# Splitting G where it is made: two fp32r parts in DRAM instead of one fp32 tile, in a Winograd feed-forward layer

## The chip, the cores and the metric

The kernel runs on one core of one Trainium2 chip. The metric is the device time of one execution in microseconds (us). Five engines work at the same time, each through its own list of instructions in order: TensorE (PE; its weight loads are shown as PEld), VectorE (DVE), ScalarE (ACT), GpSimd (POOL) and SyncE (SP), which here only starts DMA transfers. An engine waits for another only through semaphores.

## The reference

One layer of a bidirectional encoder with 1024 tokens, model width 1024 and feed-forward width 2816, all in float32:

```python
def _swiglu(x, w_in, w_out):
    g, u = jnp.split(x @ w_in, 2, axis=-1)
    return (jax.nn.silu(g) * u) @ w_out

x = x + 1/2 * post1(SwiGLU_1(pre1(x)))
u = pre_mix(x); ...            # retention and neighbourhood attention, gated and projected
x = x + post_mix(...)
x = x + 1/2 * post2(SwiGLU_2(pre2(x)))
```

pre and post are RMS norms. The change touches the two feed-forward parts (FFN 1 and FFN 2), and in them only the product of G = silu(g) * u with w_out.

## The kernel before

**Three matmuls for one.** TensorE's inputs are fp32r, a rounded float32. To keep float32 accuracy each operand X is split into a high part, ACT's cast h (L61), and a low part, VectorE's subtraction l = X - h (L62), and a product is three matmuls (`mm3`, L88 to L90): h with h, h with l, l with h. A 128x512 operand costs one ACT and one VectorE instruction to split. Weights are split by `piece` into a ring of buffers `wh`, `wl`, 8 of each.

**Seven products for eight.** Every large product is done on 2x2 blocks by Winograd's scheme: seven products of half size with sums of blocks as operands. `Winograd.NAMES` are the left operands: a11, a12, a22, s1, s2, s3, s4.

**First feed-forward product** (`ffn_in`, L405). For each of 22 feature tiles i, `Pairs.run` (L364) does seven products of 12 matmuls each, about 2.7 us a product; for the first few i two of the seven are done earlier ("leads"), so five are left: six such i in FFN 1, four in FFN 2. VectorE forms the weight sums (`t1` to `t4`, at L378, L379, L387, L396), ACT and VectorE split them into pieces, and VectorE evacuates the results and multiplies with the gate (L417) into `gt`, one tile [128, 1024] of G for a feature tile; `gt` has 3 buffers.

**Left factors** (`LeftFactors.__call__`, L430). After every second i, a pair of tiles (j of 11), POOL makes the four sums and differences of G's blocks (L440) in buffers `cmb`, 4 of them, and stores all seven left operands, 128x512 float32, 256 KB each, by DMAs from its own queue (L68) to DRAM, `gl[n][:, j * 512:(j + 1) * 512]`.

**Second feed-forward product** (`ffn_out`, L507). 7 products by 11 blocks of the feature axis are 77 steps of 12 matmuls. A step needs one block of G's left operand and one weight piece. The block comes by `Blocks`:

```python
        r = p.tile([P, 512], F32, tag="graw", name="graw", bufs=self.raws[p is not self.pools[0]])
        self.c.nc.sync.dma_start(r, src)
        a = [p.tile([P, 512], F32R, tag=g, name=g, bufs=self.pools.count(p)) for g in ("gh", "gl")]
        self.c.split(*a, r)
```

that is a load of 256 KB into one of four `graw`, and a split on ACT (`gh`) and VectorE (`gl`) into one of four pairs. The weights come as whole quadrants (`x`, 768 or 1024 KB a DMA, L521) on the same SP queue; POOL forms their differences (`sub`, L537, 55 in each FFN), and `piece` splits them. The order of the steps is written out: at step n the code asks for the operands of steps n and n + 1; how far the engines run ahead is set by the numbers of buffers. At the end of each row of blocks an epilogue (L468 to L503) normalises on ACT, VectorE and POOL beside the next steps; in FFN 1 it also transposes the result for the mixing part (tiles `pt`).

Around these the kernel has stages that the change does not touch but for the number of weight buffers: the mixing input products, attention and retention, and the output projections.

Of the kernel before, what the change touches and what calls it, by code (L numbers as in the profile page):

```python
# [10 lines left out]
F32 = mybir.dt.float32  # L11
F32R = mybir.dt.float32r
AF = mybir.ActivationFunctionType
ALU = mybir.AluOpType
# [4 lines left out]
P = 128  # L19
# [5 lines left out]
FT = DFF // P  # L25
# [13 lines left out]
class Core:  # L39
# [6 lines left out]
    def __init__(self, tc, const, wpool, psum, dram):  # L46
        self.tc, self.nc = tc, tc.nc
        self.const, self.wpool, self.psum, self.dram = const, wpool, psum, dram
        nc = self.nc
        self.ident = const.tile([P, P], F32, name="ident")  # L50
        make_identity(nc, self.ident)
        self.mhalf = const.tile([P, 8], F32, name="mhalf")
        nc.gpsimd.memset(self.mhalf, -0.5)
        self.small = None
# [19 lines left out]

    def piece(self, src, eng=None):

        h = self.wpool.tile([P, 512], F32R, tag="wh", name="wh", bufs=8)
        l = self.wpool.tile([P, 512], F32R, tag="wl", name="wl", bufs=8)
        self.split(h, l, src, eng=eng)
        return h, l  # L80

# [323 lines left out]
def ffn_in(c, pairs, pool, put):  # L405

    nc = c.nc
    for i in range(FT):
        gate = [pool.tile([P, 512], F32, tag=f"c{j}", name=f"c{j}", bufs=2) for j in range(2)]
        gt = pool.tile([P, S], F32, tag="gt", name="gt", bufs=3)  # L410
        up = gt[:, :512], gt[:, 512:]

        def done(j):
            if j < 2:
                nc.scalar.activation(gate[j], gate[j], AF.Silu)  # L415
            if j in (1, 2):
                nc.vector.tensor_tensor(up[j % 2], gate[j % 2], up[j % 2], ALU.mult)  # L417
        pairs.run(i, (*gate, *up).__getitem__, done)
        put(i, gt)


class LeftFactors:
# [1 line left out]

    order = [j + h * FT // 2 for j in range(FT // 2) for h in range(2)]

    def __init__(self, c, tmp, dst):
        self.c, self.tmp, self.dst = c, tmp, dst

    def __call__(self, i, gt):  # L430
        c, eng, j = self.c, self.c.nc.gpsimd, i // 2
        if i % 2 == 0:
            self.a11, self.a21 = gt[:, 512:], gt[:, :512]
            return
        a11, a21, a12, a22 = self.a11, self.a21, gt[:, 512:], gt[:, :512]
        s = [self.tmp.tile([P, 4, P], F32, tag="cmb", name="cmb", bufs=4).rearrange("p k t -> p (k t)")
             for _ in range(4)]
        for o, a, b, op in ((0, a21, a22, ALU.add), (2, a11, a21, ALU.subtract), (1, a22, s[2], ALU.subtract),
                            (3, a12, s[1], ALU.subtract)):
            eng.tensor_tensor(s[o], a, b, op)  # L440
        for n, a in zip(Winograd.NAMES, (a11, a12, a22, *s)):
            c.store(self.dst[n][:, j * 512:(j + 1) * 512], a)


class Blocks:


    def __init__(self, c, pools, raws):

        self.c, self.pools, self.raws, self.n = c, pools, raws, 0  # L450

    def __call__(self, src):
        p = self.pools[self.n % len(self.pools)]
        self.n += 1
        r = p.tile([P, 512], F32, tag="graw", name="graw", bufs=self.raws[p is not self.pools[0]])
        self.c.nc.sync.dma_start(r, src)
        a = [p.tile([P, 512], F32R, tag=g, name=g, bufs=self.pools.count(p)) for g in ("gh", "gl")]
        self.c.split(*a, r)
        return a


class Epilogue:
# [44 lines left out]
def ffn_out(c, tiles, q, blocks, w_out, gl, ep, side={}):  # L507
# [6 lines left out]
    later, rest, flips, xs = [], [], [], {}  # L514
# [101 lines left out]
    raws = []  # L616
# [8 lines left out]
    operands, banks, last = {}, {}, []  # L625
# [6 lines left out]
    def operand(n):  # L632
        if n < len(steps) and n not in operands:
            i, k = steps[n]
            operands[n] = blocks(gl[products[i][0]][:, k * 512:(k + 1) * 512]), c.piece(products[i][1](k))

    def one(u, k, a, b):
        c.mm3(banks[u], [p[:, u * P:(u + 1) * P] for p in a], b, k == 0, k == NK - 1)
# [1 line left out]
    for n, (i, k) in enumerate(steps):  # L640
# [11 lines left out]
        if later and i > 3:  # L652
            f = later.pop(0)
# [372 lines left out]
def trunk_layer(ctx: ExitStack, tc, x, g1a, w1i, w1o, g1b, gma, wmt, wnv, wrv, logits, dtab, rope, bias,  # L1026
# [11 lines left out]
    def dt(name, shape):  # L1038
        return dram.tile(shape, F32, name=name)

    gl = [{n: dt(f"g{i}{n}", [P, FT // 2 * 512]) for n in Winograd.NAMES} for i in range(2)]
    x1, x2 = dt("x1", [S, D]), dt("x2", [S, D])
    d = {
        "a21": dt("a21", [P, 4, 512]),
# [28 lines left out]
        fin.lead(lambda: early.tile([P, 512], F32, tag="lead", name="lead", bufs=6), on_pool=(3, 4, 5, 0))  # L1073
    g0 = pool(left, "gl10")
    with tc.tile_pool(name="fin1", bufs=1) as fp:
        ffn_in(c, fin, fp, LeftFactors(c, early, gl[0]))
    right.close()

    spool = pool(left, "s1")
# [9 lines left out]
    q = [p.tile([P, 4, 512], F32, tag="x", name="q", bufs=n) for p, n in ((ep, 2), (ep, 2), (spool, 8), (spool, 8))]  # L1089
    ahead = {}  # L1090
    fo = Epilogue(c, ep, g1b, gma, rows(x), rows(x1), wx.put)
    rest = ffn_out(c, [[b11, b12], [b21, b22]], q, Blocks(c, (g0, g1, g1, g1), (1, 3)), w1o, gl[0], fo,
                   {n: (lambda j=j: ahead.update({j: c.load_w(wnv[j])})) for j, n in enumerate((65, 66))})
    g_stack.close()
    wx.tmp = pool(g_stack, "cmb1")
# [53 lines left out]
    for f, k in zip(rest, FLIP_FILL):  # L1149
        fill(k)  # L1150
        f = f()
# [167 lines left out]


    with tc.tile_pool(name="fin2", bufs=1) as fp:
        ffn_in(c, fin, fp, LeftFactors(c, cmb, gl[1]))
    left.close()
    a_stack.close()
    g_stack.close()
# [2 lines left out]
             for _ in range(2)]  # L1328
    with tc.tile_pool(name="out2", bufs=1) as op:
        q = [op.tile([P, 4, 512], F32, tag="q", name="q", bufs=4) for _ in range(4)]  # L1330
        ffn_out(c, tiles, q, Blocks(c, (g0, g1, g0, g1), (2, 2)), w2o, gl[1],
                Epilogue(c, op, g2b, None, rows(x2), rows(out), None))
    right.close()

# [77 lines left out]
```

## Time and profile before

| what | value |
|---|---|
| median of 3 runs | 2324.83 us (2323.96 to 2324.98) |
| profiled execution | 2322.93 us, its span 2321.1 us |
| mean granted TensorE clock | 0.990 |
| TensorE busy | 2227.8 us, 96% of the span |
| VectorE / ACT / POOL busy | 1742.1 / 1003.5 / 746.3 us |
| moved by DMA | 361.25 MB, 156 GB/s on average |

Stages, in us from the start of the span: norm and leads to 69; first product of FFN 1 to 456; its second product to 690; mixing, attention, retention and output projections to 1687; first product of FFN 2 to 2087; its second product to 2313; end at 2321.

How to read the profile: a group's row gives line, engine, operation, the tiles (out<-in), shapes, count, then busy time, mean ns of one, and after the second bar the time that the engine was idle just before them with what ended it. A wait row says which engine and line waited for which, in us in total, how often, and the longest. A timeline row is start, length, engine, line, operation, tiles. A matmul of 512 columns starts about 0.23 us after the one before it.

### The profile page before, as it was taken

Reading aid. Unit: us, or ns where it says so; the run is one execution under the profiler, and the core shown is the slowest. Engines: PE = TensorE matmul, PEld = TensorE weight load, DVE = VectorE, ACT = ScalarE, POOL = GpSimd, SP = SyncE. Lnnn points to the kernel's source line nnn. Section 1 sums busy time; section 2 is a strip of 40 time slices with the busy share of each in tenths; the row PEclk is TensorE's granted clock in tenths of the full one; section 3 lists DMA queues with packets and bytes.
Section 4 is the critical chain, followed back from the end, with each engine's and each line's share of the span. In section 5 each row is a group of like instructions: output and inputs, shape, how many; then the busy total and the mean of one; then the engine's idle time right before and its main releaser. Section 6 shows DMA issues by size and latency. Waiting matters only on the chain.

```text
span 2321.1 us, 29919 instructions
## 1 busy us (share of the span) xinstructions
PE 2227.8 (96%) x10288; PEld 1837.5 (79%) x10288; DVE 1742.1 (75%) x2833; ACT 1003.5 (43%) x2102; POOL 746.3 (32%) x735
## 2 busy tenths in 40 slices
PE   6999999999998999999999999999799999999998
PEld 5788888787786887778888888887578888887776
DVE  7886666689778768869875678547887666668976
ACT  6332222353454323248885675226533233324443
POOL 5232222278424134411101222101523131316942
PEclk9999999999998999999999999999899999999999
DMA  4332323374335542257745567766433232328443
GB/s 145 116 137 101 119 94 115 131 282 152 107 114 172 175 161 100 103 177 247 221 159 176 164 217 237 283 217 213 146 114 118 96 114 95 114 88 326 120 138 122
DMA packets 135896, 361.25 MB, mean 156 GB/s; under 512 B 16000, under 2 KB 43776, under 8 KB 133632
## 3 DMA queue, kind: packets, MB, share of 16 engines
q1 hardware_dynamic: 109344, 271.76, 36.4%
q0 software_dynamic: 26400, 87.58, 10.0%
q8 instruction: 81, 1.33, 0.2%
q14 instruction: 71, 0.58, 0.1%
HBM read 263.33 MB, written 100.14 MB: 157 GB/s over the span
## 4 chain that ended last, share of the span: by engine, by line
PE 72%; DVE 13%; issue 6%; POOL 4%; DMA 3%; ACT 2%; POOLq 0%; DVEq 0%; SPq 0%; ACTq 0%
PE ps L90 22%; PE ps L88 22%; PE ps L89 22%; DVE wl L62 3%; DVE gl L62 2%; PE pt L88 1%; PE pt L89 1%; DMA wraw<-in_dram 1%; PE pt L90 1%; DVE tmp L118 1%; POOL rstd L98 1%; POOL cmb L288 1%; PE ps L741 1%; PE pt L760 1%; POOL q L482 1%
## 5 line engine op out<-in xcount | busy, mean ns | idle before, releaser
L62 DVE TENSOR_TENSOR wl<-wraw,wh 128x512 fp32r<-128x512 f32 x516 | 381.3, 762 | 79.0 <-ACT wh L61 78.1
L61 ACT CAST wh<-wraw 128x512 fp32r<-128x512 f32 x524 | 300.7, 618 | 202.9 <-DVE wraw L396 65.6
L90 PE MATMUL ps<-wh,gl 128*128 128x512 f32 x612 | 241.7, 399 | 17.0 <-DVE gl L62 16.6
L88 PE MATMUL ps<-wh,gh 128*128 128x512 f32 x612 | 240.9, 395 | 7.0 <-ACT gh L61 5.8
L89 PE MATMUL ps<-wl,gh 128*128 128x512 f32 x612 | 240.3, 394 | 2.0 <-DVE wl L62 2.0
L62 DVE TENSOR_TENSOR gl<-graw,gh 128x512 fp32r<-128x512 f32 (+2 forms) x178 | 182.7, 1030 | 74.8 <-ACT gh L61 74.7
L61 ACT CAST gh<-graw 128x512 fp32r<-128x512 f32 (+2 forms) x178 | 106.6, 601 | 210.7 <-PE ps L89 57.5
L537 POOL TENSOR_TENSOR x<-x 128x512 f32<-128x512 f32 x110 | 182.7, 1688 | 37.5 <-DMA x<-in_dram 26.7
L415 ACT ACTIVATE c<-c 128x512 f32<-128x512 f32 x88 | 55.7, 633 | 294.6 <-DVE c L385 195.2
L62 DVE TENSOR_TENSOR wl<-x,wh 128x512 fp32r<-128x512 f32 x146 | 169.2, 1169 | 7.0 <-ACT wh L61 6.9
L90 PEld LDWEIGHTS ps<-wh,gl 128*128 128x128 f32 x612 | 115.9, 190 | 52.0 <-DVE gl L62 28.5
L88 PEld LDWEIGHTS ps<-wh,gh 128*128 128x128 f32 x612 | 115.7, 189 | 34.2 <-ACT gh L61 9.3
L89 PEld LDWEIGHTS ps<-wl,gh 128*128 128x128 f32 x612 | 116.1, 190 | 26.2 <-DVE wl L62 2.7
L61 ACT CAST wh<-t 128x512 fp32r<-128x512 f32 x58 | 36.1, 622 | 200.3 <-DVE t L379 200.3
L90 PE MATMUL ps<-a12h,wl 128*128 128x512 f32 x280 | 109.9, 393 | 3.7 <-DVE wl L62 3.7
L88 PE MATMUL ps<-a11h,wh 128*128 128x512 f32 x280 | 111.8, 399 | 1.4 <-ACT wh L61 0.7
L90 PE MATMUL ps<-a11h,wl 128*128 128x512 f32 x280 | 110.6, 395 | 0.7 <-DVE wl L62 0.7
L89 PE MATMUL ps<-a11l,wh 128*128 128x512 f32 x280 | 110.6, 395 | 0.0
L88 PE MATMUL ps<-a12h,wh 128*128 128x512 f32 x280 | 110.3, 394 | 0.0
L68 POOL DMA_DIRECT2D g1a<-gt x33 | 18.1, 548 | 286.5 <-DVE gt L417 286.5
L88 PE MATMUL ps<-a22h,wh 128*128 128x512 f32 x280 | 109.7, 392 | 0.0
L89 PE MATMUL ps<-a12l,wh 128*128 128x512 f32 x280 | 109.2, 390 | 0.0
(359 smaller groups left out, 6196.6 us busy)
## 6 DMA issues: line engine op xcount, KB each, us to landing
wraw<-in_dram SPq DMA_DIRECT2D x221, 512.0 KB, 4.4
x<-in_dram SPq DMA_DIRECT2D x16, 1024.0 KB, 7.0
g0s<-cmb POOLq DMA_DIRECT2D x44, 256.0 KB, 2.7
graw<-g0s SPq DMA_DIRECT2D x44, 256.0 KB, 2.8
g1s<-cmb POOLq DMA_DIRECT2D x44, 256.0 KB, 2.7
graw<-g1s SPq DMA_DIRECT2D x44, 256.0 KB, 2.8
bt<-in_dram SPq DMA_DIRECT2D x24, 384.0 KB, 4.1
g0a<-gt POOLq DMA_DIRECT2D x33, 256.0 KB, 2.4
```

Of the source, the lines that this page charges most:

```text
L61: nc.scalar.copy(h, src)
L62: (eng or nc.vector).tensor_tensor(l, src, hf, ALU.subtract)
L88: mm(ps, a[0], b[0], start=start, stop=False)
L89: mm(ps, a[0], b[1], start=False, stop=False)
L90: mm(ps, a[1], b[0], start=False, stop=stop)
L98: self.nc.gpsimd.tensor_tensor(r[:, :n], ms, self.mhalf[:, :n], ALU.pow)
L118: nc.vector.scalar_tensor_tensor(xn[:, bs], x[:, bs], r[:, 0:1], gain[:, bs], op0=ALU.mult, op1=ALU.mult)
L288: nc.gpsimd.tensor_tensor(s3, h2, s3, ALU.subtract)
L415: nc.scalar.activation(gate[j], gate[j], AF.Silu)
L482: (eng or c.nc.gpsimd).tensor_tensor(h if out is None else out, h, self.post[:, b * 512:(b + 1) * 512], ALU.mult)
L537: e = nc.gpsimd.tensor_tensor(out, a, b, ALU.subtract).ins
L741: nc.tensor.matmul(bv, q[:, rg * P:(rg + 1) * P], k, start=n == 0, stop=n == 1)
```

## The change

`LeftFactors` splits each of the seven left operands itself: ACT copies it, rounded, into a new ring `gth` of four buffers, VectorE subtracts in place, and POOL's queue stores both parts, 14 stores a pair instead of 7, in the order a11, s1, s3, a22, s2, a12, s4. In DRAM a block of a left operand is now [128, 1024], high part and low part side by side. `Blocks` loads both parts with one DMA of 512 KB into one of seven buffers and splits nothing. The weight rings `wh` and `wl` have 7 buffers instead of 8, everywhere in the kernel.

```diff
@@ -74,8 +74,8 @@
 
     def piece(self, src, eng=None):
 
-        h = self.wpool.tile([P, 512], F32R, tag="wh", name="wh", bufs=8)
-        l = self.wpool.tile([P, 512], F32R, tag="wl", name="wl", bufs=8)
+        h = self.wpool.tile([P, 512], F32R, tag="wh", name="wh", bufs=7)
+        l = self.wpool.tile([P, 512], F32R, tag="wl", name="wl", bufs=7)
         self.split(h, l, src, eng=eng)
         return h, l
 
@@ -424,8 +424,9 @@
 
     order = [j + h * FT // 2 for j in range(FT // 2) for h in range(2)]
 
-    def __init__(self, c, tmp, dst):
-        self.c, self.tmp, self.dst = c, tmp, dst
+    def __init__(self, c, tmp, parts, dst):
+
+        self.c, self.tmp, self.parts, self.dst = c, tmp, parts, dst
 
     def __call__(self, i, gt):
         c, eng, j = self.c, self.c.nc.gpsimd, i // 2
@@ -438,25 +439,30 @@
         for o, a, b, op in ((0, a21, a22, ALU.add), (2, a11, a21, ALU.subtract), (1, a22, s[2], ALU.subtract),
                             (3, a12, s[1], ALU.subtract)):
             eng.tensor_tensor(s[o], a, b, op)
-        for n, a in zip(Winograd.NAMES, (a11, a12, a22, *s)):
-            c.store(self.dst[n][:, j * 512:(j + 1) * 512], a)
+
+        a = dict(zip(Winograd.NAMES, (a11, a12, a22, *s)))
+        for n in ("a11", "s1", "s3", "a22", "s2", "a12", "s4"):
+            h = self.parts.tile([P, 512], F32R, tag="gth", name="gth", bufs=4)
+            l = a[n].bitcast(F32R)
+            c.nc.scalar.copy(h, a[n])
+            c.nc.vector.tensor_tensor(l, a[n], h.bitcast(F32), ALU.subtract)
+            for q, p in enumerate((h, l)):
+                c.store(self.dst[n][j][:, q * 512:(q + 1) * 512], p.bitcast(F32))
 
 
 class Blocks:
 
 
-    def __init__(self, c, pools, raws):
-
-        self.c, self.pools, self.raws, self.n = c, pools, raws, 0
+    def __init__(self, c, pools):
+
+        self.c, self.pools, self.n = c, pools, 0
 
     def __call__(self, src):
         p = self.pools[self.n % len(self.pools)]
         self.n += 1
-        r = p.tile([P, 512], F32, tag="graw", name="graw", bufs=self.raws[p is not self.pools[0]])
-        self.c.nc.sync.dma_start(r, src)
-        a = [p.tile([P, 512], F32R, tag=g, name=g, bufs=self.pools.count(p)) for g in ("gh", "gl")]
-        self.c.split(*a, r)
-        return a
+        a = p.tile([P, 2, 512], F32, tag="g", name="g", bufs=self.pools.count(p))
+        self.c.nc.sync.dma_start(a.rearrange("p q t -> p (q t)"), src)
+        return [a[:, q].bitcast(F32R) for q in range(2)]
 
 
 class Epilogue:
@@ -632,7 +638,7 @@
     def operand(n):
         if n < len(steps) and n not in operands:
             i, k = steps[n]
-            operands[n] = blocks(gl[products[i][0]][:, k * 512:(k + 1) * 512]), c.piece(products[i][1](k))
+            operands[n] = blocks(gl[products[i][0]][k]), c.piece(products[i][1](k))
 
     def one(u, k, a, b):
         c.mm3(banks[u], [p[:, u * P:(u + 1) * P] for p in a], b, k == 0, k == NK - 1)
@@ -1038,7 +1044,7 @@
     def dt(name, shape):
         return dram.tile(shape, F32, name=name)
 
-    gl = [{n: dt(f"g{i}{n}", [P, FT // 2 * 512]) for n in Winograd.NAMES} for i in range(2)]
+    gl = [{n: dram.tile([FT // 2, P, 1024], F32, name=f"g{i}{n}") for n in Winograd.NAMES} for i in range(2)]
     x1, x2 = dt("x1", [S, D]), dt("x2", [S, D])
     d = {
         "a21": dt("a21", [P, 4, 512]),
@@ -1073,7 +1079,7 @@
         fin.lead(lambda: early.tile([P, 512], F32, tag="lead", name="lead", bufs=6), on_pool=(3, 4, 5, 0))
     g0 = pool(left, "gl10")
     with tc.tile_pool(name="fin1", bufs=1) as fp:
-        ffn_in(c, fin, fp, LeftFactors(c, early, gl[0]))
+        ffn_in(c, fin, fp, LeftFactors(c, early, fp, gl[0]))
     right.close()
 
     spool = pool(left, "s1")
@@ -1089,7 +1095,7 @@
     q = [p.tile([P, 4, 512], F32, tag="x", name="q", bufs=n) for p, n in ((ep, 2), (ep, 2), (spool, 8), (spool, 8))]
     ahead = {}
     fo = Epilogue(c, ep, g1b, gma, rows(x), rows(x1), wx.put)
-    rest = ffn_out(c, [[b11, b12], [b21, b22]], q, Blocks(c, (g0, g1, g1, g1), (1, 3)), w1o, gl[0], fo,
+    rest = ffn_out(c, [[b11, b12], [b21, b22]], q, Blocks(c, (g0, *[g1] * 6)), w1o, gl[0], fo,
                    {n: (lambda j=j: ahead.update({j: c.load_w(wnv[j])})) for j, n in enumerate((65, 66))})
     g_stack.close()
     wx.tmp = pool(g_stack, "cmb1")
@@ -1319,7 +1325,7 @@
 
 
     with tc.tile_pool(name="fin2", bufs=1) as fp:
-        ffn_in(c, fin, fp, LeftFactors(c, cmb, gl[1]))
+        ffn_in(c, fin, fp, LeftFactors(c, cmb, fp, gl[1]))
     left.close()
     a_stack.close()
     g_stack.close()
@@ -1328,7 +1334,7 @@
              for _ in range(2)]
     with tc.tile_pool(name="out2", bufs=1) as op:
         q = [op.tile([P, 4, 512], F32, tag="q", name="q", bufs=4) for _ in range(4)]
-        ffn_out(c, tiles, q, Blocks(c, (g0, g1, g0, g1), (2, 2)), w2o, gl[1],
+        ffn_out(c, tiles, q, Blocks(c, (g0, g1, g0, g1, g0, g1, g1)), w2o, gl[1],
                 Epilogue(c, op, g2b, None, rows(x2), rows(out), None))
     right.close()
```

## The prediction

> **What bounds the kernel now.** I read the page first, for the engine that is full and for the price of one operation; then TensorE's waits, cut at the stages that the change touches; then the windows, to see which engine stands behind each wait; then the timelines around the places where work arrives.
>
> ```profile
> span 2321.1 us, 29919 instructions
> ...
> PE 2227.8 (96%) x10288; PEld 1837.5 (79%) x10288; DVE 1742.1 (75%) x2833; ACT 1003.5 (43%) x2102; POOL 746.3 (32%) x735
> ...
> L62 DVE TENSOR_TENSOR gl<-graw,gh 128x512 fp32r<-128x512 f32 (+2 forms) x178 | 182.7, 1030 | 74.8 <-ACT gh L61 74.7
> L61 ACT CAST gh<-graw 128x512 fp32r<-128x512 f32 (+2 forms) x178 | 106.6, 601 | 210.7 <-PE ps L89 57.5
> ...
> g0s<-cmb POOLq DMA_DIRECT2D x44, 256.0 KB, 2.7
> ```
>
> TensorE is the bound, 96% busy, so the change can only win what TensorE waits for the split of G, and lose what it makes TensorE wait for elsewhere. The profiled execution took 2322.93 us, 1.8 more than its span; the median of the runs is 2324.83, 1.9 above it. I add my sum to both alike. A measurement of this kernel can tell about 0.2%, 4.65 us, from no change.
>
> TensorE's waits in the middle of the two second products (470 to 625 us, 2100 to 2250), then at their first steps (455 to 470, 2086 to 2100); columns are total, times, longest:
>
> ```profile
> PE ps L90 <- DVE gl L62: 5.6, 8, 2.1
> PE ps L88 <- ACT gh L61: 1.5, 1, 1.5
> ...
> PE ps L90 <- DVE gl L62: 7.5, 9, 2.1
> PE ps L88 <- ACT gh L61: 1.5, 1, 1.5
> ...
> PE ps L90 <- DVE gl L62: 1.3, 1, 1.3
> PE ps L88 <- ACT gh L61: 1.2, 1, 1.2
> ...
> PE ps L90 <- DVE gl L62: 1.4, 1, 1.4
> PE ps L88 <- ACT gh L61: 1.2, 1, 1.2
> ```
>
> So nothing but G's split stalls TensorE there. Windows (length; busy us of PE, PEld, DVE, ACT, POOL; granted clock, DMA share, GB/s):
>
> ```profile
> 72.00:455.00 383.00, 382.63 (x1688) 316.51 (x1687) 275.44 (x421) 118.14 (x206) 96.09 (x111) 1.00 0.33 114
> 464.00:472.00 8.00, 8.00 (x33) 6.49 (x32) 6.16 (x10) 3.83 (x7) 1.58 (x4) 0.88 1.01 396
> 480.00:560.00 80.00, 78.17 (x339) 62.77 (x339) 79.69 (x56) 37.45 (x68) 73.02 (x44) 1.00 0.59 202
> 470.00:625.00 155.00, 147.81 (x633) 118.48 (x632) 133.02 (x117) 68.68 (x129) 111.99 (x69) 0.99 0.53 176
> 2100.00:2250.00 150.00, 140.85 (x606) 112.54 (x605) 128.39 (x110) 64.42 (x118) 107.89 (x67) 1.00 0.56 188
> ```
>
> From 480 to 560 VectorE is the full engine (79.69 of 80). The first product of the FFN (72 to 455), which gets the work, leaves TensorE 0.4 us idle in 383 and VectorE 107. On averages the move is free there; the start of that stage decides.
>
> **Part 1, the split leaves the second product.** 77 casts and 77 subtractions per FFN go. What TensorE gets back is its idle time of the two middle windows: 155.00 - 147.81 = 7.2 and 150.00 - 140.85 = 9.2. Each of the 19 waits also hides 0.16, since a matmul shows 0.39 us but starts 0.23 after the last (rows at 249.49 and 249.94 below: two starts, 0.45): 3.0. And one stretch of halved clock follows a wait (chain of waits):
>
> ```profile
> 568.62 0.43 PE ps L88
> ...
> 571.18 0.43 PE pt L88
> ...
> 572.65 0.23 PE ps L90
> ```
>
> Seven matmuls from the first row to the second take 0.43 instead of 0.23: 1.4, call it 1.5. Sum 20.9. With 28 of its 56 operations gone from the 480 to 560 window, VectorE cannot fill it. What is late next is ACT, held by the epilogue's normalisation around 600 and 2230; the weight pieces, now 7 deep, cover 6 steps of 2.73 us (12 matmuls by 0.2275), 16 us. I leave 2 there: **gain 19** (bounds 10 and 21).
>
> The Trainium skill, page "TensorE: Matmul & The Clock Gate", section "Why this matters for your kernels", asks only for no idle gap over about 3 us. The longest wait ahead of the rows above is 2.1, and the clock halved all the same, so the trace decides. By the page the 1.5 would not be gained and the sum would be that much higher.
>
> **Part 2, the split arrives in the first product.** Per pair of feature tiles ACT gets 7 copies (0.60), VectorE 7 subtractions, POOL's queue 14 stores in place of 7. On average 4.2 us per 38 us on VectorE: free. But the copies go through a ring of 4 (`gth`): the sixth (a12) waits until the store of s1's high part has landed, the seventh (s4) until that of s3's has. In the order of the changed program the first pairs have these copies on ACT, and their subtractions on VectorE, ahead of the weight work that TensorE needs next. The first pair, POOL, VectorE, TensorE:
>
> ```profile
> 100.91 2.94 POOL L440 TENSOR_TENSOR cmb<-gt 128x512 f32<-128x512 f32 x2 [1.03 <-DVE gt L417]
> 103.78 0.56 POOL L68 DMA_DIRECT2D g0a<-gt  x1
> 104.36 1.30 POOL L440 TENSOR_TENSOR cmb<-gt,cmb 128x512 f32<-128x512 f32 x1
> 110.36 0.68 DVE L62 TENSOR_TENSOR wl<-t,wh 128x512 fp32r<-128x512 f32 x1
> 110.11 0.39 PE L88 MATMUL ps<-s2h,wh 128*128 128x512 f32 x1
> 111.09 0.50 PE L90 MATMUL ps<-s2h,wl 128*128 128x512 f32 x1 [0.37 <-DVE wl L62]
> ```
>
> There is no slack even now: the last row waits 0.37. After: s1 and s3 end at 103.8, s2 at 105.1; store of s1's high part, s4's subtraction, two stores (0.56 + 1.3 + 2 x 0.56) bring the store of s3's high part to 108.1; it lands 2.7 later, 110.8; copy 111.4; VectorE's subtraction 112.1; t2 112.7; its cast 113.3. TensorE wanted it at 110.11: **3.2 late**. The second pair:
>
> ```profile
> 127.25 3.00 POOL L440 TENSOR_TENSOR cmb<-gt 128x512 f32<-128x512 f32 x2 [1.18 <-DVE gt L417]
> 132.98 0.39 PE L90 MATMUL ps<-a22h,wl 128*128 128x512 f32 x1
> 138.42 0.39 PE L90 MATMUL ps<-s2h,wl 128*128 128x512 f32 x1
> ```
>
> It starts 3.2 later, 130.45. s1's store is issued 4.2 after that and lands at 137.35; copy, subtraction, one evacuation and the a22 weight's split (0.6 each) end at 139.8; wanted at 132.98 + 3.2 = 136.2: **3.6**. s3's store lands at 140.35; copy, subtraction and eight VectorE operations lead to t2's low part at about 147.0, wanted at 138.42 + 6.8 = 145.2: **1.8**. Together 8.6, and two stretches of halved clock, since waits of this size brought one above: 3. In the second FFN one early pair (subtractions from 1718.8, wanted at 1730) is late by 1 to 3: 2. **Cost 14** (bounds 6 and 18).
>
> In the steady part a pair has room:
>
> ```profile
> 229.91 3.37 POOL L440 TENSOR_TENSOR cmb<-gt 128x512 f32<-128x512 f32 x2 [1.05 <-DVE gt L417]
> 249.49 0.39 PE L88 MATMUL ps<-s2h,wh 128*128 128x512 f32 x1
> 249.94 0.39 PE L90 MATMUL ps<-s2h,wl 128*128 128x512 f32 x1
> ```
>
> By the same steps (subtractions to 235.8, three stores to 237.5, landing 240.2, copy, subtraction, three VectorE operations, cast) the cast ends at 243.9, 5.6 ahead of 249.49: no cost.
>
> **Part 3, twice the bytes, at the worst moment.** G is written and read as 512 KB a block: in the 480 to 560 window one block a step adds 0.262 MB per 2.73 us, 96 GB/s to 202; no bound. At the start of the second product the queues are full already (396 GB/s above). Issues there, 450 to 520 us, with KB and median landing; then the chain's row of the first wait:
>
> ```profile
> x<-in_dram SPq DMA_DIRECT2D x6, 1024.0 KB, 6.1
> graw<-g0a SPq DMA_DIRECT2D x9, 256.0 KB, 5.7
> g0s<-cmb POOLq DMA_DIRECT2D x4, 256.0 KB, 7.1
> ...
> 458.90 0.63 ACT gh L61
> ```
>
> The present waits of the first steps stay: block 1 lands about 1.5 later (0.262 MB more, and more behind it) and saves its split (0.60 + 0.68). New is the queue behind. Step 6 would start at 458.9 + 5 x 2.73 + 3 of waits = 475.5; its data must have left by 473.4 (2.1 of a landing is not transfer: 2.7 less 0.262 MB at 400 GB/s). By then SP must have brought blocks 1 to 6 (3.15 MB) and three weight tiles issued before (2.89): 6.03 MB. From 456.4 the queues carry 6.8, so loads alone fit. But the last pair's 13 remaining stores, 3.41 MB, come in from 461. If they take half while queued, loads carry 4.6 x 0.4 + 12.4 x 0.2 = 4.3 MB, 1.7 short: 4.6 us more at half rate, then 2 at full, 6.6 late. If loads went first: 0. Four stores landed in 7.1, that is 1.05 MB in 5 us of transfer, half of 0.4; so I stand near the upper end: 5 in each FFN. **Cost 10** (bounds 0 and 16).
>
> The Trainium skill, page "DMA: Bandwidth & Descriptors", section "Specifications", gives a core about 358 GB/s of HBM. The 396 measured is above it, so I use 400; by the page step 6 would be some 2 us later still in each FFN, and the sum 4 higher.
>
> Weight pieces 7 deep instead of 8 elsewhere: I take 0 (bounds -1 and +3), as none of the waits above names wh or wl.
>
> **Sum:** -19 + 14 + 10 = +5: profiled 2328, median **2330**.
>
> **The rivals.**
> *Loads win at the start.* Stores yield and part 3 costs nothing: -19 + 14 = -5, 2320. For it: blocks are asked for 7 ahead. Against: the 7.1 us landings.
> *The ring is free sooner.* If a store frees its buffer 1.0 us after its issue, when it has been read, and not 2.7, then each of the four delays above shrinks by up to 1.7 and part 2 costs 6: -3, 2322. For it: the copy needs the buffer, not the arrival. Against: the wait in the program is for the whole store.
> *Stores are quick*, the other side of the sign: both of these together, by one mechanism, stores that neither hold the ring nor take their half of the queue: -19 + 6 = -13, **2312**. It decides from two points: s4's copy done by 109.7 instead of 111.4, and the 13 stores behind the loads of step 6.
> *The ring stalls every pair.* If landing grows from 2.7 beyond 8.3 (2.7 + 5.6), each us past that counts once for some 18 steady pairs: one us gives +5 + 18, 2348. For it: 7.1 in the crowded stretch. Against: DMA share 0.33 from 72 to 455.
> *The middle stays bound.* G's low part is only the last of a queue behind VectorE and POOL (73 of 80 busy); then wl is late next and half the gain is lost: +14, 2339. Against: 53 subtractions leave that window.
>
> **How the numbers follow.** Forecast 0.50, loads win 0.18, ring free sooner 0.08, stores quick 0.06, every pair 0.09, middle bound 0.09. My forecast's own range is 2322 to 2338; of its 0.50 I count 0.27 slower by over 0.2%, 0.20 within, 0.03 faster. Of loads win and ring free sooner (0.26) 0.12 faster, 0.11 within, 0.03 slower; stores quick faster; the last two slower. Faster 0.21, same 0.31, slower 0.48. Range 2312 to 2346: it leaves out the far ends of "stores quick" and of "every pair".
>
> **What would show it.** Right: no TensorE wait on G's parts from 480 to 625, VectorE near 50 of 80 from 480 to 560; waits on wh or wl of 3 us near 110 and 136; waits on a G block or its weight near 470 to 480 with landings of G and its stores over 7 us. Wrong: no wait over 1 us from 100 to 150 (part 2), first steps as now (part 3), waits on wl from 540 to 570 (part 1), or waits repeating every 38 us.

## The result, and the profile after

| | median | runs | ratio to before, 95% interval |
|---|---|---|---|
| before | 2323.96 us | 9 (2320.84 to 2326.18) | |
| changed | 2333.73 us | 9 (2328.31 to 2340.19) | 1.0042 (1.003 to 1.0055) |

The changed kernel is slower by 0.42%, 9.8 us. Its profiled execution took 2335.32 us, 1.6 above its median; the span is 12.1 us longer than before's. First the page, the lines that answer to those of before:

```profile
span 2333.2 us, 30479 instructions
...
PE 2230.0 (96%) x10288; PEld 1839.0 (79%) x10288; DVE 1677.9 (72%) x2833; ACT 1010.2 (43%) x2102; POOL 806.1 (35%) x889
...
DMA packets 148220, 442.03 MB, mean 189 GB/s; under 512 B 18465, under 2 KB 46241, under 8 KB 145953
...
x<-in_dram SPq DMA_DIRECT2D x16, 1024.0 KB, 12.2
g0s<-gth POOLq DMA_DIRECT2D x44, 256.0 KB, 4.1
```

VectorE does the same 2833 instructions in 64 us less, POOL 60 us more, the DMA 81 MB more; TensorE's share is what it was. Sums of the page do not say where 12 us went. Both programs issue 10288 matmuls, in an order that differs only locally, so the k-th matmul of one can be set against the k-th of the other. The table gives, for every kernel run, how much longer than before's profile each stretch took, in us, between matmuls 200, 1900, 2200, 2700, 3100, 7700, 9300, 9600 and 10200 (first product of FFN 1; start and middle of its second product; its end; everything between the FFNs; the same of FFN 2) and from there to the end of the span.

| kernel | first 1 | start 1 | middle 1 | end 1 | between | first 2 | start 2 | middle 2 | last |
|---|---|---|---|---|---|---|---|---|---|
| changed | +11.9 | +7.5 | -14.0 | +1.4 | +7.6 | +3.1 | +1.3 | -10.1 | +3.4 |
| e1 ring free | +14.9 | +6.4 | -14.0 | +2.3 | +8.1 | +5.1 | +2.0 | -10.1 | +3.4 |
| e2 split on POOL | +15.5 | +7.3 | -14.0 | +2.5 | +3.2 | +8.6 | +0.3 | -10.1 | +3.4 |
| e3 last low parts early | +13.2 | +1.7 | -14.0 | +3.1 | +2.3 | +4.5 | +0.6 | -10.1 | +3.4 |
| e4 before, 7 buffers | -0.5 | +0.6 | -2.9 | +0.5 | +3.3 | 0.0 | -1.1 | -0.4 | 0.0 |
| e5 before, no low part | -0.7 | -2.2 | -14.2 | 0.0 | -0.6 | 0.0 | -4.5 | -9.3 | +0.1 |
| e6 no early subtraction | -0.6 | +6.4 | -14.0 | +1.3 | +7.8 | 0.0 | +1.8 | -10.1 | +3.4 |
| e7 raw pairs | -0.6 | +7.0 | -14.0 | +2.7 | +2.7 | 0.0 | +1.8 | -10.1 | +0.1 |
| e8 raw pairs and a11 | -0.6 | +4.5 | -14.0 | -0.3 | +3.9 | 0.0 | -0.4 | -10.1 | +0.1 |
| e9 the same, 8 buffers | -0.5 | +5.4 | -14.0 | -0.4 | -2.9 | +1.4 | +1.4 | -10.1 | +0.1 |
| e10 four split pairs | -0.5 | +4.7 | -13.7 | +7.6 | +3.8 | 0.0 | -0.1 | -10.1 | +4.1 |
| e11 the same, 8 buffers | 0.0 | +4.7 | -13.9 | +0.9 | -4.7 | 0.0 | +2.7 | -1.4 | +4.1 |
| e12 before again | -0.6 | +2.2 | -0.7 | -0.3 | -1.2 | 0.0 | +0.4 | 0.0 | 0.0 |

The last row is the scale: two profiles of before differ by up to 2.2 in a stretch, and by 0.1 in all. Each row is one execution, and not always a middling one: those of e1 and e6 took 7.1 and 3.8 us more than the medians of their kernels, that of e9 3.6 less. In the changed kernel the middles give back 24.1, and seven other stretches take 36.2. TensorE's waits in the changed kernel, middle of FFN 1's second product with its start (470 to 640 us):

```profile
PE ps L88 <- DMA g<-g0a: 6.4, 3, 2.6
PE ps L127 <- issue: 1.5, 1, 1.5
PE ps L88 <- ACT gth L447: 0.8, 1, 0.8
PE ps L88 <- ACT wh L61: 0.6, 1, 0.6
```

No wait on the split of a loaded block of G is left (the row with gth is the copy of the last pair); loads of G have taken its place. The window that answers to 480 to 560 of before (there VectorE was busy 79.69 of 80 with 56 operations, the queues at 202 GB/s):

```profile
490.00:570.00 80.00, 76.78 (x324) 62.98 (x325) 32.90 (x29) 21.46 (x36) 62.28 (x44) 0.96 0.90 347
```

VectorE fell to 33 of 80, with half the operations (the prediction said near 50; a weight split also got shorter, 1169 ns on average against 1334 from 470 to 625 before), and the queues went from 0.59 to 0.90 of their time. TensorE was busy 1.4 us less than before in this window, which begins inside the start with its waits on loads. In the first product of FFN 1, VectorE and then TensorE (timelines):

```profile
101.12 0.69 DVE L448 TENSOR_TENSOR gt<-gt,gth 128x512 fp32r<-128x512 f32 x1 [1.06 <-POOL cmb L441]
101.73 3.62 DVE L448 TENSOR_TENSOR cmb<-cmb,gth 128x512 fp32r<-128x512 f32 x2
105.28 0.68 DVE L448 TENSOR_TENSOR gt<-gt,gth 128x512 fp32r<-128x512 f32 x1
105.88 0.68 DVE L448 TENSOR_TENSOR cmb<-cmb,gth 128x512 fp32r<-128x512 f32 x1
106.48 0.68 DVE L385 TENSOR_TENSOR c<-ps,c 128x512 f32<-128x512 f32 x1
107.08 0.68 DVE L448 TENSOR_TENSOR gt<-gt,gth 128x512 fp32r<-128x512 f32 x1
107.68 0.68 DVE L390 TENSOR_TENSOR c<-ps,gt 128x512 f32<-128x512 f32 x1
...
110.08 0.67 DVE L448 TENSOR_TENSOR cmb<-cmb,gth 128x512 fp32r<-128x512 f32 x1
110.68 0.68 DVE L379 TENSOR_TENSOR t<-wraw 128x512 f32<-128x512 f32 x1
...
112.12 0.50 PE L88 MATMUL ps<-s2h,wh 128*128 128x512 f32 x1 [1.90 <-ACT wh L61]
...
139.70 0.79 PE L90 MATMUL ps<-a22h,wl 128*128 128x512 f32 x1 [3.57 <-DVE wl L62]
```

TensorE waits where the prediction had it wait (112 and 136 to 140). But from 105.28 on VectorE starts an operation every 0.60 us, without idle time (no brackets behind these rows): the last subtraction (110.08) and the t2 behind it (110.68) came when their turn came, not when a store had landed.

### The profile page after: what moved, and what is told of

It is laid out like the page before. It is cut to its first block, busy times and chain, and to the rows that moved or that the text cites. A ratio compares the mean times of both kernels' runs of the same rounds, so it can differ in the third digit from the quotient of the medians.

```text
span 2333.2 us, 30479 instructions
## 1 busy us (share of the span) xinstructions
PE 2230.0 (96%) x10288; PEld 1839.0 (79%) x10288; DVE 1677.9 (72%) x2833; ACT 1010.2 (43%) x2102; POOL 806.1 (35%) x889
## 3 DMA queue, kind: packets, MB, share of 16 engines
q0 software_dynamic: 38720, 127.96, 14.7%
## 4 chain that ended last, share of the span: by engine, by line
PE 59%; issue 13%; DVE 12%; POOL 6%; DMA 6%; ACT 3%; POOLq 0%; SPq 0%; DVEq 0%; ACTq 0%
PE ps L90 18%; PE ps L88 18%; PE ps L89 18%; DVE wl L62 3%; POOL cmb L441 2%; DMA g1s<-gth 1%; DMA g<-g0a 1%; PE pt L89 1%; PE pt L90 1%; PE pt L88 1%; DMA wraw<-in_dram 1%; ACT wh L61 1%; POOL rstd L98 1%; DVE tmp L118 1%; DVE t L379 1%
## 5 line engine op out<-in xcount | busy, mean ns | idle before, releaser
L62 DVE TENSOR_TENSOR wl<-x,wh 128x512 fp32r<-128x512 f32 x146 | 137.8, 956 | 192.1 <-ACT wh L61 191.0
L88 PE MATMUL ps<-wh,g 128*128 128x512 f32 x484 | 191.5, 397 | 11.3 <-DMA g<-g0a 6.4
L89 PE MATMUL ps<-wl,g 128*128 128x512 f32 x484 | 191.1, 395 | 0.0
L90 PE MATMUL ps<-wh,g 128*128 128x512 f32 x484 | 190.4, 393 | 0.0
L61 ACT CAST wh<-x 128x512 fp32r<-128x512 f32 x146 | 88.6, 620 | 216.4 <-PE pt L90 93.0
L441 POOL TENSOR_TENSOR cmb<-gt 128x512 f32<-128x512 f32 x44 | 63.7, 1464 | 320.6 <-DVE gt L417 320.6
L543 POOL TENSOR_TENSOR x<-x 128x512 f32<-128x512 f32 x110 | 158.8, 1469 | 34.2 <-DMA x<-in_dram 24.2
L88 PEld LDWEIGHTS ps<-wh,g 128*128 128x128 f32 x484 | 92.2, 191 | 33.4 <-ACT wh L61 7.4
L90 PE MATMUL ps<-a22h,wl 128*128 128x512 f32 x280 | 110.3, 394 | 3.6 <-DVE wl L62 3.6
L89 PE MATMUL ps<-a22l,wh 128*128 128x512 f32 x280 | 109.8, 392 | 0.0
L89 PEld LDWEIGHTS ps<-wl,g 128*128 128x128 f32 x484 | 92.3, 191 | 20.1 <-DVE wl L62 1.2
```

The lines of the kernel that those rows point to most:

```text
L61: nc.scalar.copy(h, src)
L62: (eng or nc.vector).tensor_tensor(l, src, hf, ALU.subtract)
L88: mm(ps, a[0], b[0], start=start, stop=False)
L89: mm(ps, a[0], b[1], start=False, stop=False)
L90: mm(ps, a[1], b[0], start=False, stop=stop)
L543: e = nc.gpsimd.tensor_tensor(out, a, b, ALU.subtract).ins
```

## The experiments

**Is it the ring?** e1 takes the ring's waits out of the early pairs, e2 takes two of the splits off ACT and VectorE.

```diff
# e1: in three early pairs the store reads the low part, not the ring's buffer
-            for q, p in enumerate((h, l)):
+            for q, p in enumerate((l if j < 3 and n in ("a11", "s1", "s3") else h, l)):
```

> The changed kernel, but in the first three pairs of each FFN the DMAs that stored the high parts of a11, s1 and s3 store the low part in their place: same bytes, same queue, but no store holds a buffer of the ring of four any more, so the copies of a12 and s4 wait for no landing (the stored values of these blocks are thereby not the high parts). Theory (the ring): the time that the first product of FFN 1 lost against before (+11.9 us by TensorE's matching instructions) falls to 0 to 4, that of FFN 2 (+3.1) to 0 to 1, the rest stays: some 10 us faster than the changed kernel. Rival (the seven added subtractions on VectorE, 4.2 us a pair, are in front of the weights): +11.9 stays at 8 or more. Second rival (twice the DMA issues on POOL's queue): stays as well.

```diff
# e2
+            if n in ("a12", "s4"):
+                eng.tensor_copy(h, a[n])                       # eng: POOL
+                eng.tensor_tensor(l, a[n], h.bitcast(F32), ALU.subtract)
+            else: ...                                          # as changed
```

> The changed kernel, with the copy and the subtraction of a12 and s4 moved from ACT and VectorE to POOL, so that only POOL's own list waits for the ring. Theory (the ring holds up ACT and VectorE in front of the weights): first product of FFN 1 from +11.9 to +1 to +4, of FFN 2 from +3.1 to 0 to +1, about 10 us faster than the changed kernel, 2321 to 2326. Rival (VectorE's five remaining subtractions do it): +8 or more stays. Price to watch: POOL's added 2 copies and 2 subtractions, about 5 us a pair of 38.

Measured: e1 2333.73 us (ratio to before 1.0047, 1.003 to 1.0064), e2 2338.68 (1.0061, 1.0045 to 1.0076). The loss in the first product of FFN 1 did not fall in either: +14.9 and +15.5. (e1's median is the changed kernel's; its profiled execution was its slowest, so that it lost more than the changed kernel is not shown.) TensorE's waits from 95 to 160 us, e1 and then e2, and a VectorE row of e2:

```profile
PE ps L88 <- ACT wh L61: 7.1, 4, 2.5
PE ps L90 <- DVE wl L62: 2.1, 2, 1.7
...
PE ps L90 <- DVE wl L62: 7.1, 2, 4.4
PE ps L88 <- ACT wh L61: 3.3, 2, 2.6
...
110.25 2.34 DVE L387 TENSOR_TENSOR wraw<-wraw 128x512 f32<-128x512 f32 x1
```

The waits are still for the weights behind VectorE. In e2 an operation of 0.68 us took 2.34 beside POOL's new subtraction: two splits fewer on VectorE cost it more than they saved. The Trainium skill, page "SBUF — State Buffer", section "SBUF: two separate sides", says that VectorE and GpSimd share a pair of ports which one operation holds to its end, when VectorE has two inputs in SBUF and GpSimd reads SBUF; this row and the 3.62 for two operations at 101.73, beside POOL's first subtractions, agree. So the ring fell as the cause in the first product.

**Is it VectorE's added work?**

e6 leaves out the seven subtractions of each of the first three pairs; what is stored as low part is the block as it is.

```diff
# e6
-            c.nc.vector.tensor_tensor(l, a[n], h.bitcast(F32), ALU.subtract)
+            if j >= 3:
+                c.nc.vector.tensor_tensor(l, a[n], h.bitcast(F32), ALU.subtract)
```

> The changed kernel, without the 7 VectorE subtractions in each of the first three pairs of each FFN (the block as it is is stored as the low part, so these blocks count double); ring, copies, stores, queue and bytes unchanged. The first two runs took the ring away and moved two splits to POOL, and the loss in the first product of FFN 1 rose from +11.9 to +14.8 and +15.6: the ring is not it. New theory (VectorE is full while five products a tile leave it 13.6 us a tile, 21 subtractions of 0.6 are 12.6 us and pass through to TensorE): loss falls to 0 to +3, in FFN 2 from +3.1 to 0 to +1. Rival (ACT's copies or POOL's 14 issues in front of the weights): +8 or more stays.

Measured: 2315.19 us (0.9963, 0.9951 to 0.9975). First product of FFN 1 -0.6, as in the second profile of before; of FFN 2 0.0 instead of +3.1. Windows from 100 to 150 us, before, changed, e6 (length; busy PE, PEld, DVE, ACT, POOL; clock, DMA share, GB/s):

```profile
100.00:150.00 50.00, 49.63 (x220) 40.76 (x219) 47.76 (x70) 17.32 (x30) 17.86 (x21) 1.00 0.45 158
...
100.00:150.00 50.00, 42.12 (x168) 32.52 (x166) 42.24 (x63) 20.01 (x35) 24.98 (x35) 0.93 0.56 202
...
100.00:150.00 50.00, 50.00 (x223) 41.40 (x222) 45.29 (x68) 24.76 (x44) 23.32 (x35) 1.00 0.61 214
```

e6 keeps the ring, the copies and all 14 stores of a pair, and loses nothing. This settles part 2: the subtractions, in a stretch in which VectorE had 2.2 of 50 us left. The expectation's 12.6 us, for 21 subtractions, is near the 11.9 by chance. In the changed kernel's timeline only 14 of them, 8.4 us at 0.60, fall in this stretch (101 to 110 and 132 to 141); those of the third pair, from 169.7 on, come after TensorE's lag has reached its 11.9. VectorE, which works in order, also stands idle ahead of each of the two groups until POOL has made its operand (1.06 us in the row at 101.12, 1.69 at 131.81). That makes 9.0 us more than it had free, an estimate from these rows. The five gaps between TensorE's matmuls that grew most grew by 8.6 in all; the other 3.3 are mostly matmuls at a lower granted clock (0.93 in the window).

**Is it the bytes at the start of the second product?** e3 moves the stores of the last pair's low parts five pairs earlier, with that pair's values.

> The changed kernel, with the low parts of the last pair not stored at the end of the first product (1.8 MB less there; the bytes are written five pairs earlier, with that pair's values, so the last block's low parts are not the right ones). Theory (stores and loads share a full queue at the start of the second product): the loss there, +7.5 us in FFN 1 against before, falls to +2 to +5; waits on loads of G near 487 and 497 shrink. Rival (the loads alone, 512 instead of 256 KB, are too many): stays at +6 or more. Second rival (the last pair's copies on ACT hold up the weights): the ring turns faster with fewer stores and some of it goes too, but the waits would name the weights' casts, not G's loads.

Measured: 2328.84 us (1.0025, 1.0016 to 1.0034); start +1.7 instead of +7.5, in FFN 2 +0.6 instead of +1.3. Landings of the changed kernel from 455 to 520, a step of its chain of waits, then TensorE's waits from 456 to 505, changed and e3:

```profile
g<-g0a SPq DMA_DIRECT2D x10, 512.0 KB, 15.8
g0s<-gth POOLq DMA_DIRECT2D x4, 256.0 KB, 10.0
...
477.13 23.11 DMA g<-g0a
...
PE ps L88 <- DMA g<-g0a: 6.4, 3, 2.6
PE ps L88 <- ACT gth L447: 0.8, 1, 0.8
...
PE ps L88 <- DMA g<-g0a: 4.1, 4, 1.4
PE ps L88 <- ACT gth L447: 0.8, 1, 0.8
```

A block of G that takes 23 us from issue to landing outruns seven blocks of prefetch (19 us). With 1.8 MB less in the queue the same block takes 18.8, the longest wait falls from 2.6 to 1.4 us, and the granted clock from 480 to 520 is 1.00 instead of 0.91. So stores do hold loads up. But with no more bytes of stores than before, G's blocks still take up to 18.8 us, against 9.2 before, and the median of g0a hardly moves (15.8 to 14.7): the larger part of the long landings goes with the doubled loads.

In FFN 2 the longest wait at the start, 2.8 us, is another one. ACT, TensorE and the ring of four at the last pair there:

```profile
2117.79 0.62 ACT L447 CAST gth<-gt 128x512 fp32r<-128x512 f32 x1 [6.88 <-DMA g1s<-gth]
2118.31 2.17 ACT L61 CAST wh<-x 128x512 fp32r<-128x512 f32 x4
...
2118.98 0.80 PE L88 MATMUL ps<-wh,g 128*128 128x512 f32 x1 [2.79 <-ACT wh L61]
```

ACT stood idle for 6.9 us until a store of a copy had landed, and the weight's cast behind it came late. This is the step that the prediction saw in the first product; it happened here, where stores are slow. No run took the ring away at the last pair alone; e1 frees it in the first three.

**What is the middle worth?** e5, on before, leaves out the subtraction that makes G's low part; the high part stands in for it.

```diff
# e5
-        a = [p.tile([P, 512], F32R, ...) for g in ("gh", "gl")]
-        self.c.split(*a, r)
-        return a
+        a = [p.tile([P, 512], F32R, ...) for g in ("gh",)]
+        self.c.nc.scalar.copy(a[0], r)
+        return a * 2
```

> The kernel before, without the subtraction that makes G's low part (the high part is used in its place, so the products are not the right ones); load, copy, eight weight buffers and all stores as before. Theory (VectorE's subtraction of G is what the middle of the second products waited for): against before -13 to -15 in the middle of FFN 1's second product and -9 to -11 in FFN 2's, as the changed kernel has (-14.0 and -10.1), and nothing lost in the first products: 2296 to 2302. Rival (the shorter chain of loads and copies did it too): less than -10 and -7. Between the FFNs it tells how far two profiles with eight weight buffers differ: if within 2 us, the 5 to 8 us that the changed kernels lose there belong to seven buffers; if 3 or more, they are scatter. The last drain of POOL stays at 4.1 us.

Measured: 2291.38 us (0.9857, 0.9842 to 0.9872). Middles -14.2 and -9.3, against -14.0 and -10.1 of the changed kernel; ACT's copy and the load are still there. So it was VectorE's subtraction alone that TensorE waited for. It is also faster at the start in FFN 2 (-4.5; the -2.2 in FFN 1 is within the scatter), which put it below the expected range.

**Do seven weight buffers cost anything?**

```diff
# e4, on before
-        h = self.wpool.tile([P, 512], F32R, tag="wh", name="wh", bufs=8)     # and wl
+        h = self.wpool.tile([P, 512], F32R, tag="wh", name="wh", bufs=7)
```

> The kernel before with 7 instead of 8 buffers in the weight rings, nothing else. The prediction took 0 (-1 to +3) for this. If it is the cause of the 7 to 8 us that the changed kernel's profile lost between the two FFNs (about +0.3 near 1000 to 1100 us, +6 between 1390 and 1500), the same loss shows in these places and the time is 5 to 10 us above before. If those were the disturbance of one run, the time is within 3 us of before and the loss is elsewhere or gone.

> The kernel before, unchanged, profiled a second time: how far two profiles of one kernel differ stage by stage. If the stretch between the FFNs differs by less than 2 us, the 3 to 8 us of the kernels with seven weight buffers are no scatter; the first products and the middles of the second products should agree within 0.5 us.

Measured: e4 2324.41 us (1.0007, 0.9998 to 1.0016): within the scatter as a whole. e12, one execution, 2322.82. But in the column "between", all nine kernels with seven buffers lose 2.3 to 8.1 us, and the five with eight stand at 0 (before), -0.6, -1.2, -2.9 and -4.7. TensorE's waits from 1000 to 1500 us, changed, then e4, then before again:

```profile
PE ps L747 <- ACT qh L64: 4.2, 1, 4.2
PE pt L766 <- DVE s L756: 3.9, 3, 2.0
PE ps L88 <- DVE sb L928: 1.8, 1, 1.8
PE pt L968 <- ACT yn L959: 1.6, 1, 1.6
...
PE pt L760 <- DVE s L750: 4.0, 3, 2.1
PE ps L741 <- ACT qh L64: 1.4, 1, 1.4
PE pt L962 <- ACT yn L953: 1.2, 1, 1.2
...
PE ps L741 <- ACT qh L64: 3.2, 1, 3.2
PE pt L760 <- DVE ptl L62: 1.6, 2, 0.8
PE pt L760 <- DVE s L750: 1.2, 2, 0.8
```

e4 differs from before by the buffers alone, and it has the changed kernel's longer waits for `s` and its wait for `yn`; so have all nine, and none of the five. None of these waits names wh or wl: why a smaller ring of weights makes `s` and `yn` late in attention and retention was not followed up. The place repeats: between matmuls 6400 and 7000 (1410 to 1532 us) all nine lose 2.6 to 6.8 us and the other four 0 to 0.3. So the buffers cost something there, 2.9 us in e4 and 6.8 in the changed kernel; the rest of the column is within what kernels with equal buffers differ by. By time alone e4 cannot tell its part from no change.

**Can it be had without the costs?** e7 stores the pairs that cost (0, 1, 2 and 10) unsplit and splits their blocks in the second product; e8 does so with a11 too; e9 is e8 with eight weight buffers.

```diff
# e7; e8 adds: or n == "a11"
+def unsplit(n, j):
+    return j in (0, 1, 2, 10)
# LeftFactors
+            if unsplit(n, j):
+                c.store(self.dst[n][j][:, :512], a[n])
+                continue
# Blocks
+        if raw:
+            self.c.nc.sync.dma_start(a[:, 1], src[:, :512])
+            self.c.split(*hl, a[:, 1])
# e9: e8 with wh, wl bufs=8, gth bufs=2, Blocks of six buffers
```

> The changed kernel, but pairs 0, 1, 2 and 10 of each FFN are stored unsplit, 7 stores, and their four blocks of each product are loaded as 256 KB and split in the second product, as before; the other seven pairs as changed. The results are the right ones. Theory (VectorE is full early, the queues are full at the last pair, VectorE has room in the middle now): first product of FFN 1 0 to +2, start of its second product 0 to +3, middle -11 to -14, in FFN 2 0, 0 to +2, -8 to -10; 5 +- 3 between the FFNs, and at the end POOL's last drain, which went from 4.14 to 7.98 us with 154 more DMAs on its queue, at 6.6 with 98 more: in all -8 to -14 against before, 2310 to 2316, faster than both. Rival (splits in the middle bring back the waits on G's low part): middle -7 and -5, 2320 or more.

> As the kernel with raw pairs, and also a11 is stored unsplit in all pairs, so that the first product of the second matmul loads 256 KB a block and splits it there, where VectorE has room and the queues have none. Theory (bytes at the start): a start another 0 to 2 us shorter than with raw pairs alone, POOL's last drain 6.2 us, 1 to 3 us faster in all. Rival (the start is at before's level already with raw pairs, and the added splits put VectorE behind): same or slower by up to 2.

> The kernel with raw pairs 0, 1, 2, 10 and a11 raw, with the weight rings back at eight buffers; the room comes from the ring of the copies, two instead of four, and from G's blocks, six deep instead of seven. Right results. Theory (seven weight buffers cost 3 to 8 us between the FFNs): that stretch from +4.0 to 0 to +2, 2 to 4 us faster than with seven; the ring of two costs nothing, as the ring of four did not. Rival (the 4.0 are scatter): the same time within 1.5. Second rival (the ring of two now holds up ACT in front of the weights): a wait in every pair from 190 us on, slower by 5 or more.

Measured: e7 2312.53 us (0.9949, 0.9936 to 0.9961), e8 2308.13 (0.9928, 0.9915 to 0.994), e9 2306.5 (0.9924, 0.991 to 0.9937). All three beat both kernels, e9 by 0.76% against before. The first products lose nothing, the middles keep all of -14.0 and -10.1 although 4 of 11 blocks are split there again. The start was expected at 0 to +3 in e7 and is +7.0. TensorE's waits from 455 to 525, e7 and then e8; then e9's window:

```profile
PE ps L90 <- DVE g L62: 4.3, 3, 2.7
PE ps L88 <- ACT g L61: 3.2, 2, 2.1
PE ps L88 <- DMA g<-g0a: 0.4, 1, 0.4
...
PE ps L90 <- DVE g L62: 4.8, 6, 1.4
PE ps L88 <- ACT g L61: 0.7, 1, 0.7
...
490.00:570.00 80.00, 76.23 (x336) 62.48 (x335) 59.35 (x47) 25.74 (x45) 70.13 (x46) 1.00 0.70 256
```

The waits on loads turned into waits on splits: the first three blocks are now raw, and the split at the start comes last again, as before. e9 has its time between the FFNs back (-2.9, in an execution 3.6 us below its median), and a ring of two cost nothing in the first product of FFN 1 and 1.4 in that of FFN 2 (0.0 in e11). e8 and e9 ran against different runs of before, and their intervals overlap: that eight buffers are better here is shown by the stretch, not by the time.

**How few pairs are enough?** e10: only pairs 3, 5, 7 and 9 split, a11 never; e11: the same with eight buffers, a ring of two and six blocks.

> Only pairs 3, 5, 7 and 9 are stored split (and a11 never), all other blocks of G are loaded as 256 KB and split in the second product; seven weight buffers. Right results. Theory (the middle only needs VectorE relieved below what TensorE asks; with 4 of 11 blocks unsplit the gain was the whole -14.0 and -10.1): with 7 of 11 unsplit VectorE has 20 splits fewer than before in 55 steps of five products, so the gain in the middle shrinks only a little, -10 to -14 and -7 to -10, while fewer bytes shorten the start by 0 to 2: same as with 7 split pairs within 3 us. Rival (any run of unsplit blocks brings the waits back): half the gain, 6 to 12 us slower.

> As the kernel with four split pairs, with eight weight buffers, a ring of two and six blocks of G. Theory (seven buffers cost 3 to 8 us between the FFNs): 2 to 4 us faster than with seven. Rival (scatter): the same within 1.5 us. The stretch between the FFNs against before: 0 to +2 by the theory, +3 or more if the buffers are not it.

Measured: e10 2317.67 us (0.9967, 0.9955 to 0.998), e11 2315.06 (0.9959, 0.9946 to 0.9971). e10's middles keep their gain (-13.7 and -10.1) as the theory has it, but it is 9.5 us slower than e8 against the 3 expected: it lost +7.6 at the end of FFN 1's second product, with one more wait of 3.2 us there, of a transpose for the epilogue's square on ACT, which writes to the same tile (`pt`), and +4.1 after the last matmul. That wait and what follows it made 5.2 us by the next long one (e8 has lost 0.3 there); the rest of the 7.6 was not followed up. e11 loses FFN 2's middle (-1.4), in one wait, and a halved clock behind it (waits from 2150 to 2300):

```profile
PE ps L88 <- ACT g L61: 4.6, 1, 4.6
PE ps L90 <- DVE g L62: 0.8, 1, 0.8
```

The expected reasons were right for neither kernel as a whole. That four split pairs leave too little margin is a guess; no run varied it further.

## Why the prediction was right, and where it was not

It forecast 2330 with a range of 2312 to 2346 and slower as the likeliest; measured 2333.73. That the two lie so close is in part luck: the gain came out 5 us larger, and 12 us of loss had no term in the sum or a term of 0. Its terms, against the changed kernel's profile:

| term | predicted | measured |
|---|---|---|
| part 1, the two middles | -19 | -24.1 |
| part 2, the two first products | +14 | +15.0 |
| part 3, the two starts | +10 | +8.8 |
| weight buffers, between the FFNs | 0 (-1 to +3) | +7.6 |
| end of FFN 1's second product | not in the sum | +1.4 |
| after the last matmul | not in the sum | +3.4 |

- **Part 1** was right in kind (e5), too small: beyond its upper bound of 21. It counted the waits of two windows and gave 2 back for ACT's epilogue; that wait did not come in either middle, and the stretches measured here also hold the transposes at 630, with a halved clock behind them in before's profile and none after. The table's stretches also begin elsewhere than the prediction's windows (526 and 2146 us in before), so the two columns match only roughly.
- **Part 2** had a right number for a wrong reason. The step that failed is "the copies go through a ring of 4": delays of 3.2, 3.6 and 1.8 were derived from stores that had to land, and 2.6, 4.1 and 2.4 were found at these places, but e1 and e6 show that the stores had no part in it. What was late is VectorE's own list: two pairs' subtractions, 8.4 us, and its idle time ahead of them, against 2.2 free in the window above. That 8.6 us of delays and 3 of slow clock were forecast and 8.6 and 3.3 found is luck. The ring did hold ACT up, but at the last pair, at the start of the second product (6.9 us in FFN 2).
- **Part 3** was right in kind (e3, and landings over 7 us, as announced). FFN 1 lost 7.5, above the forecast, FFN 2 only 1.3, because there the waits of before at the start went away at the same time; the longest that is left there stands behind the ring and not behind a load. That the present waits would stay was wrong: in the changed kernel none on a split of a loaded block is left there.
- **Weight buffers** is the term that was mis-sized: 0, where nine profiles show 2.3 to 8.1 between the FFNs. "None of the waits above names wh or wl" was no sign: it looked at other stages, and where the time was lost no wait names them either.
- Of the rivals, the faster one (stores quick) and "the ring stalls every pair" rested on the ring and fell with it. The first sign of "stores quick" did come, s4's copy was done by 109.5, since the pair began 2.4 us earlier; TensorE waited all the same. From matmul 600 to 1900, the steady part, the changed kernel lost 0.0. "Loads win at the start" fell with the landings of 10 to 16 us. "The middle stays bound" fell: -24.1.
- The Trainium skill, page "TensorE: Matmul & The Clock Gate", section "Why this matters for your kernels", asks for no idle gap over about 3 us. Shorter gaps were enough in the changed kernel, where the clock halved after gaps of 2.6 and 2.8 us between matmuls at 488 and 497. A gap of 2.9 at 491 in e9 brought no slower matmul, so the length of a gap alone does not decide. The changed kernel's rows behind the second gap (chain of waits):

```profile
500.37 0.62 PE ps L88
500.99 0.43 PE ps L89
501.42 0.43 PE ps L90
```

## What to carry to other kernels

Price moved work in the stage that receives it, at that stage's tightest stretch, not by the stage's mean: VectorE had 107.6 of 383 us free in the first product and 2.2 of 50 where the work arrived first. A mechanism derived from an instruction order can give the right number and still be the wrong one; look for what runs without a gap (VectorE, every 0.60 us) before blaming what is waited for. Move only as much as is needed: splitting seven of eleven pairs early kept the whole gain, and the pairs that collide with a full engine or a full queue stayed as they were. A ring that costs nothing where stores land in 3 to 4 us can hold its engine up where they take 10.

## What was not expected of the hardware

After the last matmul the changed kernel took 3.4 us longer. Its work ends as in before; what is late is POOL's drain at the end of the program, the last thing that the closing barrier waits for. In the traces it took, by the number of DMA instructions on POOL in the trace:

| DMAs of POOL | 314 | 362 | 398 | 412 | 468 |
|---|---|---|---|---|---|
| last drain, us | 4.14 | 8.72 | 2.02 | 3.17 | 7.98 |
| kernels | before, e4, e5, e12 | e10, e11 | e8, e9 | e7 | changed, e1, e2, e3, e6 |

It repeats to 0.01 us in kernels with the same number, and grows by 0.08 us a DMA from 398 to 412 and by 0.09 on to 468, but it does not grow with the number throughout: the 6.6 and 6.2 us expected for e7 and e8, from 314 and 468 by a straight line, were 3.17 and 2.02. Up to about 4 us it lies beside the last output stores and costs nothing. What sets it was not tried.
